# The last stage of a streaming block: two odd inner tiles moved from the first group to the end, and eight banks for the first up products

## The chip, the cores and the metric

The kernel runs on one core of a Trainium2 chip. The metric is device time in microseconds (us) of one execution. A core has a matrix engine (TensorE, "PE" in the profile, with its weight loads as "PEld"), three engines for elementwise work (VectorE "DVE", ScalarE "ACT", GpSimd "POOL"), and a sync engine (SP) that here issues the DMAs. PE writes only into PSUM, which has eight banks of 128 partitions by 512 float32. Data that the engines work on lies in SBUF.

## The reference

One block of a model with 1,024 tokens (plus 16 meta tokens, dropped at the end) and 1,024 channels: a mixer with two branches, and then a gated MLP with a causal depthwise convolution of width 3. The change touches the MLP only:

```python
def conv_ffn(hn, w_up, w_conv, w_down):
    u = hn @ w_up                                   # 1024 -> 2 * 2816
    u_pad = jnp.pad(u, ((0, 0), (CONV_W - 1, 0), (0, 0)))
    uc = sum(w_conv[j] * u_pad[:, j:j + length] for j in range(CONV_W))
    gate, val = jnp.split(uc, 2, axis=-1)
    return (jax.nn.silu(gate) * val) @ w_down       # 2816 -> 1024

h = h + conv_ffn(rms_norm(h, norm_ffn), ffn_up, ffn_conv, ffn_down)
return h[:, N_META:N_META + s]
```

## The kernel before

Every large product is done in float32 accuracy by three matmuls: both factors are split into a high part (rounded to the matrix engine's format) and a low part (the rest), and `mm3` (from L212) issues high x high (L218), high x low (L219) and low x high (L220) into one bank. A weight tile is split by `wload` (from L194): a DMA into `wf` (three buffers), a cast on ACT to `wh` (L205), a subtraction on POOL to `wl` (L206); `wh` and `wl` have four buffers each, and one such buffer holds four tiles of 128 by 128.

Stage 4 makes the mixer's output `h2` (eight tiles of 128 channels, held in SBUF to the end) and its normed and split form `x2`: 16 tiles, high and low for each of eight channel tiles. It does so in three windows of tokens; the last window is normed after the first two (L1038 on DVE, cast L1040 on ACT, subtraction L1041 on DVE or, for channel tiles 3 and 7, POOL).

Stage 5 is the MLP. The inner width of 2,816 is 22 tiles of 128. `up(kt)` makes one inner tile `gr`: for each of three windows of tokens a gate product and a value product (24 matmuls of 342 or 344 columns each, six products and 144 matmuls in all), each followed by the convolution (ACT L1137, DVE L1138 and L1139), Silu on ACT (L1149) and the product of both (DVE L1151). A product's bank comes free when L1139 has read it. The products use the tag `mm`, the down products the tag `dn`; `banks` says which PSUM banks a tag goes round.

Two inner tiles form a pair, and `seven_x` (ACT, DVE and POOL; L1102, L1103, L1106, L1109) makes from a pair seven left factors in the manner of Strassen: with inner tiles and output tiles taken two by two, and the tokens in two halves, seven products of 512 columns stand for eight. `seven_w` makes the weights that belong to them (adds on POOL L1076, casts on ACT L1083, subtractions on POOL L1084). `down(gi, gs, last)` adds a group's pairs into `h2`: for each of four pairs of output tiles seven products, each 3 matmuls per pair of inner tiles, and 12 additions of 128x512 on DVE (L1171). A group with one pair has 84 matmuls in its down products, a group with two pairs 168; both have 48 additions. `GS = [2, 4, 4, 4, 4, 4]` gives the inner tiles of each group: the first has one pair, the others two. A group's down products stand behind the first `up` of the next group; the last group's stand at the end, behind the last `up` and the last `seven_x`, and there each finished half of an output tile is sent out (L1176).

A scheduler fixes each engine's order when the program is built, from the written order and a modelled timeline. Each engine then works its own list strictly in order and waits on semaphores.

Of the kernel before, what the change touches and what calls it, by code (L numbers as in the profile page):

```python
# [8 lines left out]
F32R = mybir.dt.float32r  # L9
# [3 lines left out]
ALU = mybir.AluOpType  # L13
# [4 lines left out]
P = 128  # L18
D = 1024
KD = 8  # L20
SEQ = 1024
# [11 lines left out]
LT = L - T0  # L33
CW = [(14, 356), (356, 698), (698, 1040)]
CF = [(16, 356), (356, 698), (698, 1040)]
GS = [2, 4, 4, 4, 4, 4]
CHA = [(0, 348), (348, 696), (696, 1040)]
CV = [(0, 384), (384, 768), (768, 1040)]
G = [(0, 384), (384, 768), (768, 1040)]
# [154 lines left out]
def wload(S, src, kt, pool=None):  # L194

    nc = S.nc
    pool = pool or S.wp
    res = []
    for h in range(0, kt, 4):
        n = min(4, kt - h)  # L200
        wf = S.wp.tile([P, 4, P], F32, name="wf", tag="wf", bufs=3)
        nc.sync.dma_start(out=wf[:, :n], in_=src[:, h:h + n])
        wh = pool.tile([P, 4, P], F32R, name="wh", tag="wh", bufs=4)
        wl = pool.tile([P, 4, P], F32R, name="wl", tag="wl", bufs=4)
        nc.scalar.copy(out=wh[:, :n], in_=wf[:, :n])  # L205
        nc.gpsimd.tensor_tensor(out=wl[:, :n], in0=wf[:, :n], in1=wh[:, :n], op=ALU.subtract)  # L206
        for k in range(n):
            res.append((wh[:, k], wl[:, k]))
    return res


def mm3(S, ps, w, x, first=True, last=True):  # L212

    nc = S.nc
    n = len(w)
    for k in range(n):
        (wh, wl), (xh, xl) = w[k], x[k]
        nc.tensor.matmul(ps, lhsT=wh, rhs=xh, start=first and k == 0, stop=False)  # L218
        nc.tensor.matmul(ps, lhsT=wh, rhs=xl, start=False, stop=False)  # L219
        nc.tensor.matmul(ps, lhsT=wl, rhs=xh, start=False, stop=last and k == n - 1)  # L220
# [6 lines left out]
def banks(S, **use):  # L227

    S.psb.update({k: v.split() for k, v in use.items()})
    S.psn.update({k: 0 for k in use})  # L230


def slot(S, tag, name):
    w = 1024 if tag in "SM" else 512
    pool = S.pp if tag in "toAB" else S.pq
    return pool.tile([P, w], F32, name=name, tag=tag, bufs=1)


def psum(S, tag):

    slots = S.psb[tag]
    n = S.psn[tag] % len(slots)
    S.psn[tag] += 1
    t = slots[n]
    if n and slots[n - 1] == t:
        return S.half[tag][:, 512:1024]
    S.half[tag] = slot(S, t, tag)
    return S.half[tag][:, 0:512]
# [818 lines left out]
def seven_w(S, pool, w1, w2, n):  # L1067


    nc = S.nc  # L1070
    a11, a12 = w1[:, 0:2 * n:2], w1[:, 1:2 * n:2]
    a21, a22 = w2[:, 0:2 * n:2], w2[:, 1:2 * n:2]

    def add(x, y, op=ALU.add):
        t = pool.tile([P, 2, P], F32, name="ws", bufs=2)
        nc.gpsimd.tensor_tensor(out=t[:, :n], in0=x, in1=y, op=op)  # L1076
        return t[:, :n]

    def split(*src):
        wh, wl = [S.wp.tile([P, 4, P], F32R, name=nm, tag=nm, bufs=4) for nm in ("wh", "wl")]  # L1080
        for i, x in enumerate(src):
            o = slice(2 * i, 2 * i + n)
            nc.scalar.copy(out=wh[:, o], in_=x)  # L1083
            nc.gpsimd.tensor_tensor(out=wl[:, o], in0=x, in1=wh[:, o], op=ALU.subtract)  # L1084
        return [[(wh[:, 2 * i + k], wl[:, 2 * i + k]) for k in range(n)] for i in range(len(src))]

    yield from split(add(a11, a12), a22)
    yield from split(a11, add(a21, a22))
    yield from split(add(a11, a22), add(a12, a22, ALU.subtract))
    yield from split(add(a21, a11, ALU.subtract))  # L1090


def seven_x(S, g1, g2):


    nc = S.nc
    H = slice(0, 512), slice(512, 1024)
    T = lambda dt=F32R: S.xp.tile([P, SEQ], dt, name="gx", tag="x")

    def halves(g):  # L1100
        h, l = T(), T()
        nc.scalar.copy(out=h[:], in_=g[:])  # L1102
        nc.gpsimd.tensor_tensor(out=l[:], in0=g[:], in1=h[:], op=ALU.subtract)  # L1103
        return [(h[:, s], l[:, s]) for s in H]

    comb = lambda out, x, y, op=ALU.add: nc.vector.tensor_tensor(out=out, in0=x, in1=y, op=op)  # L1106
    (a, b), (c, d) = [[g[:, s] for s in H] for g in (g1, g2)]
    f = T()
    nc.scalar.copy(out=f[:, H[0]], in_=a)  # L1109
    comb(f[:, H[1]], a, f[:, H[0]], ALU.subtract)  # L1110
    u = T(F32)
    comb(u[:, H[0]], a, d)
    comb(u[:, H[1]], c, d)
    x1, x7 = halves(u)
    comb(c, c, a, ALU.subtract)
    x4, x5 = halves(g2)
    comb(a, a, b)
    comb(b, b, d, ALU.subtract)
    x6, x3 = halves(g1)
    return x5, x4, x3, (f[:, H[0]], f[:, H[1]]), x1, x7, x6  # L1120


def stage5(S):


    nc, tc = S.nc, S.tc
    banks(S, mm="0 1 2 3", dn="t o A B")
    with tc.tile_pool(name="p5", bufs=1) as p5:

        def conv(w, mt, a, z, name):  # L1130
            n = z - a
            c0 = a - 2 - T0
            ps = psum(S, "mm")
            mm3(S, ps[:, :n + 2], w, [(h[:, c0:c0 + n + 2], l[:, c0:c0 + n + 2]) for h, l in S.x2])
            cw = lambda j: S.par("conv", 44 * j + mt)
            t = p5.tile([P, 344], F32, name=name, bufs=2)
            nc.scalar.activation(out=t[:, :n], in_=ps[:, 0:n], func=AF.Identity, scale=cw(0))  # L1137
            nc.vector.scalar_tensor_tensor(out=t[:, :n], in0=ps[:, 1:1 + n], scalar=cw(1), in1=t[:, :n], op0=ALU.mult, op1=ALU.add)  # L1138
            nc.vector.scalar_tensor_tensor(out=t[:, :n], in0=ps[:, 2:2 + n], scalar=cw(2), in1=t[:, :n], op0=ALU.mult, op1=ALU.add)  # L1139
            return t  # L1140

        def up(kt):
            wg = wload(S, S.A["w_up"][kt], KD)
            wv = wload(S, S.A["w_up"][22 + kt], KD)
            gr = p5.tile([P, SEQ], F32, name="gr", bufs=2)
            for a, z in CF:
                n = z - a
                g = conv(wg, kt, a, z, "ug")
                nc.scalar.activation(out=g[:, :n], in_=g[:, :n], func=AF.Silu)  # L1149
                v = conv(wv, 22 + kt, a, z, "uv")  # L1150
                nc.vector.tensor_tensor(out=gr[:, a - N_META:z - N_META], in0=g[:, :n], in1=v[:, :n], op=ALU.mult)  # L1151
            return gr

        def down(gi, gs, last):
            k0 = sum(GS[:gi])
            n = len(gs)
            for m in range(0, KD, 2):
                wf = []
                for i in range(2):
                    w = S.wp.tile([P, 4, P], F32, name="wf", tag="wf", bufs=3)  # L1160
                    nc.sync.dma_start(out=w[:, :2 * n], in_=S.A["w_down"][m + i, :, k0:k0 + 2 * n])
                    wf.append(w)
                factors = seven_w(S, p5, wf[0], wf[1], n)
                half = lambda i, j: S.h2[m + i][:, 2 + 512 * j:514 + 512 * j]

                for j, to in enumerate((((0, 0, -1), (0, 1, 1)), ((0, 0, 1), (1, 0, 1)), ((0, 1, 1), (1, 1, 1)),
                                        ((1, 0, 1), (1, 1, -1)), ((0, 0, 1), (1, 1, 1)), ((0, 0, 1),), ((1, 1, 1),))):
                    ps = psum(S, "dn")
                    mm3(S, ps[:], next(factors), [g[j] for g in gs])
                    for r, c, sign in to:  # L1170
                        nc.vector.tensor_tensor(out=half(r, c), in0=half(r, c), in1=ps[:],  # L1171
                                                op=ALU.add if sign > 0 else ALU.subtract)
                if last:
                    for i in range(2):
                        for j in range(2):
                            nc.sync.dma_start(out=S.outT[m + i][:, 512 * j:512 * j + 512], in_=half(i, j))  # L1176

        pend = None
        kt = 0
        for gi, n in enumerate(GS):  # L1180
            gs = []
            for i in range(0, n, 2):
                g1 = up(kt)
                if i == 0 and pend is not None:
                    down(gi - 1, pend, False)
                g2 = up(kt + 1)
                kt += 2
                gs.append(seven_x(S, g1, g2))
            pend = gs
        down(len(GS) - 1, pend, True)  # L1190


def build(tc, A, outs):
# [114 lines left out]
```

## Time and profile before

| | |
|---|---|
| median of 3 runs | 1933.45 us (1931.68 to 1941.54) |
| the profiled execution | 1933.08 us, of which the span of the profile is 1930.9 us |
| PE busy | 1815.3 us, 94% of the span |
| DVE, ACT, POOL busy | 1114.6, 770.8, 766.7 us |
| mean granted TensorE clock | 0.969 |

The first up product of stage 5 starts at 1182.7 us of the span. PE is the busy engine there, so the profile is read by asking where PE, once stage 5 has begun, does not start its next matmul when it could. A matmul's own duration in the profile overlaps the next one's; what counts for throughput is the distance between starts.

### The profile page before, as it was taken

The page shows a single profiled execution, that of the slowest core. Times are in us where ns is not written, and L with a number is a line of the kernel's source. Part 1 is how long each engine was busy: PE and PEld are TensorE (multiplying, and loading weights), DVE is VectorE, ACT ScalarE, POOL GpSimd, SP SyncE. Part 2 cuts the span into 40 slices and gives each one's busy share as a digit, 9 for nine tenths or more (in the row PEclk, how much of TensorE's full clock was granted, in tenths as well). Part 3 has the DMA queues.
Part 4 walks back from the last instruction along what each step waited for, and adds up shares of the span by engine and source line. Part 5 has one row for each costly group of instructions (what it writes and reads, how often), then busy time and mean ns, then how long its engine had stood idle before and what let it go on. Part 6 is the DMA issues. An engine that isn't in the chain of part 4 may idle for free.

```text
span 1930.9 us, 33790 instructions
## 1 busy us (share of the span) xinstructions
PE 1815.3 (94%) x12744; PEld 1628.9 (84%) x12744; DVE 1114.6 (58%) x2062; ACT 770.8 (40%) x1706; POOL 766.7 (40%) x858
## 2 busy tenths in 40 slices
PE   6899999999998899999879998989999999999998
PEld 5588778788787688989769997979999899899996
DVE  6225635645727686442346447575756856757567
ACT  5345434444635432243365324333323333233232
POOL 4134224223324311232313334353744834636546
PEclk9899999899999899999989999999999999999998
DMA  5221331332413455565654332111121111211112
GB/s 183 95 71 44 83 77 55 79 88 57 112 47 90 95 138 154 156 188 160 188 147 137 111 123 84 36 53 44 44 67 44 44 46 43 66 44 44 61 39 104
DMA packets 197578, 170.84 MB, mean 88 GB/s; under 512 B 93768, under 2 KB 154744, under 8 KB 197416
## 3 DMA queue, kind: packets, MB, share of 16 engines
q1 hardware_dynamic: 197160, 168.62, 30.6%
q8 instruction: 101, 1.65, 0.4%
q14 instruction: 61, 0.50, 0.1%
q0 software_dynamic: 256, 0.07, 0.0%
HBM read 122.57 MB, written 46.06 MB: 87 GB/s over the span
## 4 chain that ended last, share of the span: by engine, by line
PE 54%; DVE 4%; DMA 2%; ACT 2%; issue 1%; POOL 1%; SPq 1%; DVEq 0%; ACTq 0%; POOLq 0%
PE mm L219 11%; PE mm L218 11%; PE mm L220 11%; PE dn L219 3%; PE dn L218 3%; PE dn L220 3%; PE gate L218 3%; PE gate L219 3%; PE gate L220 3%; DVE h L1171 1%; DMA y<-y_d 1%; DVE x L1041 1%; PE ch L541 1%; DVE x L1038 0%; PE ch L534 0%
## 5 line engine op out<-in xcount | busy, mean ns | idle before, releaser
L206 POOL TENSOR_TENSOR wl<-wf,wh 128x512 fp32r<-128x512 f32 x220 | 289.5, 1319 | 524.7 <-ACT wh L205 488.6
L218 PE MATMUL mm<-x,wh 128*128 128x344 f32 (+1 forms) x1056 | 338.3, 320 | 6.2 <-DVE ug L1139 6.2
L219 PE MATMUL mm<-x,wh 128*128 128x344 f32 (+1 forms) x1056 | 339.6, 322 | 0.0
L220 PE MATMUL mm<-x,wl 128*128 128x344 f32 (+1 forms) x1056 | 337.2, 320 | 1.0 <-POOL wl L206 1.0
L1171 DVE TENSOR_TENSOR h<-h,dn 128x512 f32<-128x512 f32 x288 | 183.3, 683 | 40.4 <-PE dn L220 32.8
L218 PEld LDWEIGHTS mm<-x,wh 128*128 128x128 f32 x1056 | 199.9, 189 | 7.1 <-ACT uv L1137 6.5
L205 ACT CAST wh<-wf 128x512 fp32r<-128x512 f32 x220 | 135.6, 617 | 164.8 <-PE mm L219 69.2
L220 PEld LDWEIGHTS mm<-x,wl 128*128 128x128 f32 x1056 | 199.4, 189 | 1.8 <-POOL wl L206 1.5
L219 PEld LDWEIGHTS mm<-x,wh 128*128 128x128 f32 x1056 | 200.0, 189 | 0.5
L218 PE MATMUL dn<-gx,wh 128*128 128x512 f32 x308 | 123.2, 401 | 11.1 <-ACT gx L1102 5.7
L218 PE MATMUL gate<-xh,wh 128*128 128x342 f32 x384 | 127.3, 332 | 4.1 <-ACT sg L856 2.1
L219 PE MATMUL gate<-xl,wh 128*128 128x342 f32 x384 | 127.3, 332 | 0.0
L220 PE MATMUL gate<-xh,wl 128*128 128x342 f32 x384 | 126.6, 330 | 0.0
L219 PE MATMUL dn<-gx,wh 128*128 128x512 f32 x308 | 122.6, 398 | 0.6 <-POOL gx L1103 0.6
L220 PE MATMUL dn<-gx,wl 128*128 128x512 f32 x308 | 122.1, 397 | 0.0
L218 PE MATMUL mm<-xh,wh 128*128 128x348 f32 (+5 forms) x336 | 116.9, 348 | 3.9 <-ACT xh L156 1.8
L219 PE MATMUL mm<-xl,wh 128*128 128x348 f32 (+5 forms) x336 | 114.4, 341 | 1.6 <-POOL xl L158 1.2
L220 PE MATMUL mm<-xh,wl 128*128 128x348 f32 (+5 forms) x336 | 112.6, 335 | 0.0
L1138 DVE SCALAR_TENSOR_TENSOR uv<-mm,par,uv 128x342 f32<-128x342 f32 (+1 forms) x66 | 37.7, 571 | 109.3 <-ACT uv L1137 109.3
L218 PE MATMUL pr<-xh,wh 128*128 128x386 f32 (+1 forms) x288 | 95.9, 333 | 1.4 <-ACT bt L469 1.4
L1084 POOL TENSOR_TENSOR wl<-ws,wh 128x256 fp32r<-128x256 f32 (+1 forms) x120 | 81.9, 694 | 33.5 <-ACT wh L1083 33.4
L219 PE MATMUL pr<-xl,wh 128*128 128x386 f32 (+1 forms) x288 | 94.8, 329 | 0.0
(317 smaller groups left out, 4333.1 us busy)
## 6 DMA issues: line engine op xcount, KB each, us to landing
wf<-in_w_up_dram SPq DMA_DIRECT2D x88, 256.0 KB, 2.7
wf<-in_w_down_dram SPq DMA_DIRECT2D x40, 256.0 KB, 2.8
sg_d<-sg SPq DMA_DIRECT2D x48, 171.0 KB, 3.4
sg<-sg_d SPq DMA_DIRECT2D x48, 171.0 KB, 2.4
wf<-in_w_gate_dram SPq DMA_DIRECT2D x32, 256.0 KB, 4.5
wf<-in_w_out_dram SPq DMA_DIRECT2D x32, 256.0 KB, 2.7
wf<-in_w_rw_dram SPq DMA_DIRECT2D x28, 256.0 KB, 2.8
wf<-in_w_qkv_dram SPq DMA_DIRECT2D x24, 256.0 KB, 2.8
```

The costliest lines, as they stand in the source:

```text
L205: nc.scalar.copy(out=wh[:, :n], in_=wf[:, :n])
L206: nc.gpsimd.tensor_tensor(out=wl[:, :n], in0=wf[:, :n], in1=wh[:, :n], op=ALU.subtract)
L218: nc.tensor.matmul(ps, lhsT=wh, rhs=xh, start=first and k == 0, stop=False)
L219: nc.tensor.matmul(ps, lhsT=wh, rhs=xl, start=False, stop=False)
L220: nc.tensor.matmul(ps, lhsT=wl, rhs=xh, start=False, stop=last and k == n - 1)
L541: nc.tensor.matmul(pz[r, q, :], lhsT=bkt[:, q, r], rhs=uv[e][:, q, :], start=True, stop=True)
L1041: (nc.gpsimd if m in (3, 7) else nc.vector).tensor_tensor(out=l[:, s], in0=x[:], in1=h[:, s], op=ALU.subtract)
L1084: nc.gpsimd.tensor_tensor(out=wl[:, o], in0=x, in1=wh[:, o], op=ALU.subtract)
L1138: nc.vector.scalar_tensor_tensor(out=t[:, :n], in0=ps[:, 1:1 + n], scalar=cw(1), in1=t[:, :n], op0=ALU.mult, op1=ALU.add)
L1171: nc.vector.tensor_tensor(out=half(r, c), in0=half(r, c), in1=ps[:], op=ALU.add if sign > 0 else ALU.subtract)
```

## The change

The group of one pair at the start goes. The first 20 inner tiles form five groups of two pairs. The last two inner tiles (20 and 21) are split into high and low as they are (`plain`) and multiplied by ordinary products (`down_last`), and their `up` calls stand ahead of the down products of the fifth group. The up products of the first two inner tiles may use all eight banks. The order in `up`, `seven_x` and `seven_w` is not touched.

```diff
-GS = [2, 4, 4, 4, 4, 4]
+GS = [4, 4, 4, 4, 4, 2]
...
-    banks(S, mm="0 1 2 3", dn="t o A B")
+    banks(S, mm="0 1 2 3 t o A B", dn="t o A B")
...
-        def down(gi, gs, last):
+        def down(gi, gs):
...
-                if last:
-                    for i in range(2):
-                        for j in range(2):
-                            nc.sync.dma_start(out=S.outT[m + i][:, 512 * j:512 * j + 512], in_=half(i, j))
+
+        def plain(g):
+
+            h, l = [S.mp.tile([P, SEQ], F32R, name="gp", tag="x2", bufs=16) for _ in range(2)]
+            nc.scalar.copy(out=h[:], in_=g[:])
+            nc.gpsimd.tensor_tensor(out=l[:], in0=g[:], in1=h[:], op=ALU.subtract)
+            return h, l
+
+        def down_last(gs):
+            for m in range(KD):
+                w = wload(S, S.A["w_down"][m, :, 20:22], 2)
+                for a in (0, 512):
+                    ps = psum(S, "dn")
+                    mm3(S, ps[:], w, [(h[:, a:a + 512], l[:, a:a + 512]) for h, l in gs])
+                    hs = S.h2[m][:, 2 + a:2 + a + 512]
+                    nc.vector.tensor_tensor(out=hs, in0=hs, in1=ps[:], op=ALU.add)
+                    nc.sync.dma_start(out=S.outT[m][:, a:a + 512], in_=hs)
...
-        for gi, n in enumerate(GS):
+        for gi in range(5):
             gs = []
-            for i in range(0, n, 2):
+            for i in range(2):
                 g1 = up(kt)
                 if i == 0 and pend is not None:
-                    down(gi - 1, pend, False)
+                    down(gi - 1, pend)
                 g2 = up(kt + 1)
                 kt += 2
                 gs.append(seven_x(S, g1, g2))
+                if kt == 2:
+                    banks(S, mm="0 1 2 3")
             pend = gs
-        down(len(GS) - 1, pend, True)
+        g1, g2 = up(20), up(21)
+        down(4, pend)
+        down_last([plain(g1), plain(g2)])
```

Three places show what the built order makes of it. First, PE at the third window of the first inner tile. `mm_13314` is its gate product, `mm_13344` its value product; x2_12045 and x2_12046 are the high and low part of channel tile 0, x2_12059 and x2_12060 of channel tile 7. Before, the end of the gate product and the start of the value product:

```order
L219 MATMUL mm_13314<-x2_12058,wh_13177 128x344
L220 MATMUL mm_13314<-x2_12057,wl_13178 128x344
L218 MATMUL mm_13314<-x2_12059,wh_13177 128x344
L219 MATMUL mm_13314<-x2_12060,wh_13177 128x344
L220 MATMUL mm_13314<-x2_12059,wl_13178 128x344
L218 MATMUL mm_13344<-x2_12045,wh_13183 128x344
L219 MATMUL mm_13344<-x2_12046,wh_13183 128x344
L220 MATMUL mm_13344<-x2_12045,wl_13184 128x344
```

And now, at the start of the gate product:

```order
L219 MATMUL mm_13284<-x2_12060,wh_13189 128x344
L220 MATMUL mm_13284<-x2_12059,wl_13190 128x344
L218 MATMUL mm_13314<-x2_12045,wh_13171 128x344
L218 MATMUL mm_13344<-x2_12045,wh_13183 128x344
L219 MATMUL mm_13314<-x2_12046,wh_13171 128x344
L220 MATMUL mm_13314<-x2_12045,wl_13172 128x344
L218 MATMUL mm_13314<-x2_12047,wh_13171 128x344
L219 MATMUL mm_13344<-x2_12046,wh_13183 128x344
L220 MATMUL mm_13344<-x2_12045,wl_13184 128x344
L218 MATMUL mm_13344<-x2_12047,wh_13183 128x344
```

The two products have moved into one another: they go through the channel tiles together, in two banks.

Second, ACT at the same place. `ug_13219` and the three below it are the first four products, read from their banks; `wh_13376` and `wh_13382` are the gate weights of the second inner tile, `wh_13388` and `wh_13394` its value weights. Before:

```order
L1040 CAST x2_12059<-x_13161 128x342
L1137 ACTIVATE ug_13219<-mm_13194,par_136 128x340
L1137 ACTIVATE uv_13249<-mm_13224,par_136 128x340
L1137 ACTIVATE ug_13279<-mm_13254,par_136 128x342
L1137 ACTIVATE uv_13309<-mm_13284,par_136 128x342
L1149 ACT_TABLE_LOAD
L1149 ACTIVATE ug_13219<-ug_13219 128x340
L1149 ACTIVATE ug_13279<-ug_13279 128x342
L1109 CAST gx_13579<-gr_13193 128x512
L205 CAST wh_13376<-wf_13374 128x512
L205 CAST wh_13382<-wf_13380 128x512
```

And now:

```order
L1040 CAST x2_12059<-x_13161 128x342
L205 CAST wh_13376<-wf_13374 128x512
L205 CAST wh_13382<-wf_13380 128x512
L1137 ACTIVATE ug_13219<-mm_13194,par_136 128x340
L1137 ACTIVATE uv_13249<-mm_13224,par_136 128x340
L1137 ACTIVATE ug_13279<-mm_13254,par_136 128x342
L1137 ACTIVATE uv_13309<-mm_13284,par_136 128x342
L1149 ACT_TABLE_LOAD
L1149 ACTIVATE ug_13219<-ug_13219 128x340
L205 CAST wh_13388<-wf_13386 128x512
L205 CAST wh_13394<-wf_13392 128x512
```

The casts of the second inner tile's gate weights have moved ahead of the first four reads of a bank.

Third, POOL around the last `up`. `wf_...` with 128x256 operands are the down weights of the first pair of output tiles. Before, with the three subtractions of `seven_x` (L1103) of the last pair:

```order
L1076 TENSOR_TENSOR ws_19872<-wf_19867 128x256
L1076 TENSOR_TENSOR ws_19898<-wf_19869 128x256
L1103 TENSOR_TENSOR gx_19752<-gx_19748,gx_19751 128x1024
L1103 TENSOR_TENSOR gx_19757<-gr_19564,gx_19756 128x1024
L1103 TENSOR_TENSOR gx_19763<-gr_19359,gx_19762 128x1024
L1084 TENSOR_TENSOR wl_19875<-ws_19872,wh_19874 128x256
L1084 TENSOR_TENSOR wl_19875<-wf_19869,wh_19874 128x256
```

And now, where those three stand an `up` pair earlier and the two subtractions of `plain` (L1178) have come in:

```order
L1084 TENSOR_TENSOR wl_19475<-wf_19441,wh_19474 128x256
L1084 TENSOR_TENSOR wl_19475<-ws_19472,wh_19474 128x256
L1178 TENSOR_TENSOR gp_19830<-gr_19055,gp_19829 128x1024
L1076 TENSOR_TENSOR ws_19500<-wf_19441,wf_19443 128x256
L1084 TENSOR_TENSOR wl_19503<-ws_19498,wh_19502 128x256
L1084 TENSOR_TENSOR wl_19503<-ws_19500,wh_19502 128x256
L1076 TENSOR_TENSOR ws_19525<-wf_19443,wf_19441 128x256
L1076 TENSOR_TENSOR ws_19543<-wf_19538 128x256
L1178 TENSOR_TENSOR gp_19834<-gr_19260,gp_19833 128x1024
L1084 TENSOR_TENSOR wl_19528<-ws_19525,wh_19527 128x256
L1084 TENSOR_TENSOR wl_19546<-ws_19543,wh_19545 128x256
```

The weights of products 0 to 3 of the first pair of output tiles stand ahead of the first L1178, those of products 4 and 5 (`wl_19503`) between the two, those of product 6 (`wl_19528`) behind the second.

## Rows read from the trace of the kernel before

**Rows 1.** PE's waits by what released them, 1175 to 1310 us: total, times, longest.
```profile
PE mm L218 <- DVE ug L1139: 6.2, 1, 6.2
PE dn L218 <- ACT wh L1083: 2.7, 4, 1.3
PE dn L218 <- DVE h L1171: 2.5, 5, 0.9
```
**Rows 2.** The same view, 1310 us to the end: its larger row of two.
```profile
PE dn L218 <- ACT gx L1102: 5.7, 2, 3.6
```
**Rows 3.** Down matmuls, 1896 to 1927 us, undisturbed: count, ns min/median/max, first and last start.
```profile
L218 PE MATMUL dn<-gx,wh x44: 388/392/399, 1895.8 to 1925.7; 128*128 128x512 f32 x44
```
**Rows 4.** Up matmuls in the same view, 1296.5 to 1380 us, undisturbed.
```profile
L218 PE MATMUL mm<-x,wh x177: 313/319/328, 1296.6 to 1379.9; 128*128 128x344 f32 x121, 128*128 128x342 f32 x56
```
**Rows 5.** PE in order of time, 1200 to 1212 us: start, duration; in brackets, idle before.
```profile
1200.62 0.32 PE L220 MATMUL mm<-x,wl 128*128 128x344 f32 x1
1207.19 0.63 PE L218 MATMUL mm<-x,wh 128*128 128x344 f32 x1 [6.25 <-DVE ug L1139]
...
1211.01 0.32 PE L219 MATMUL mm<-x,wh 128*128 128x344 f32 x1
```
**Rows 6.** All engines by stretch; the column behind POOL's is the granted clock.
```profile
1205.00:1210.00 5.00, 2.81 (x10) 2.84 (x11) 4.38 (x10) 4.05 (x7) 0.00 (x0) 0.50 0.00 0
1885.00:1890.00 5.00, 2.60 (x5) 1.27 (x5) 1.83 (x1) 1.04 (x1) 5.00 (x3) 0.50 0.00 0
```
**Rows 7.** POOL, ACT and DVE in order of time, 1203 to 1207 us.
```profile
1203.99 0.91 POOL L1041 TENSOR_TENSOR x<-x,x 128x342 fp32r<-128x342 f32 x1 [2.44 <-ACT x L1040]
...
1204.93 0.54 ACT L1137 ACTIVATE ug<-mm,par 128x340 f32<-128x340 f32 x1 [1.02 <-POOL x L1041]
...
1206.48 0.56 DVE L1139 SCALAR_TENSOR_TENSOR ug<-mm,par,ug 128x340 f32<-128x340 f32 x1
...
1206.81 1.28 ACT L1149 ACT_TABLE_LOAD   x1
```
**Rows 8.** Matmuls of the first group's down products, 1255 to 1300 us, as in rows 3.
```profile
L218 PE MATMUL dn<-gx,wh x28: 388/401/496, 1262.0 to 1293.5; 128*128 128x512 f32 x28
```
**Rows 9.** DVE's groups, 1255 to 1295 us: count, busy us, mean ns, idle before.
```profile
L1171 DVE TENSOR_TENSOR h<-h,dn 128x512 f32<-128x512 f32 x48 | 29.5, 680 | 3.1 <-PE dn L220 2.9
```
**Rows 10.** PE in order of time, 1877 us to the end.
```profile
1877.40 0.39 PE L218 MATMUL dn<-gx,wh 128*128 128x512 f32 x1
...
1926.14 0.40 PE L220 MATMUL dn<-gx,wl 128*128 128x512 f32 x1
```
**Rows 11.** DVE and POOL in order of time, 1879 to 1891 us.
```profile
1879.40 0.93 DVE L1151 TENSOR_TENSOR gr<-ug,uv 128x342 f32<-128x342 f32 x1
...
1883.76 2.52 POOL L1103 TENSOR_TENSOR gx<-gx 128x1024 fp32r<-128x1024 f32 x1 [1.70 <-ACT gx L1102]
1886.24 5.15 POOL L1103 TENSOR_TENSOR gx<-gr,gx 128x1024 fp32r<-128x1024 f32 x2
```
**Rows 12.** Groups of DVE, POOL and ACT, 1896 to 1926 us, as in rows 9.
```profile
L1171 DVE TENSOR_TENSOR h<-h,dn 128x512 f32<-128x512 f32 x38 | 24.7, 685 | 5.4 <-PE dn L220 3.8
...
L1084 POOL TENSOR_TENSOR wl<-ws,wh 128x256 fp32r<-128x256 f32 x13 | 9.5, 739 | 2.4 <-ACT wh L1083 2.4
...
L1083 ACT CAST wh<-ws 128x256 fp32r<-128x256 f32 x13 | 5.2, 406 | 14.8 <-PE dn L219 9.2 <-POOL ws L1076 5.4
```
**Rows 13.** DMA issues, 1880 us to the end: count, KB each, median us to landing.
```profile
out_dram<-h SPq DMA_DIRECT2D x16, 256.0 KB, 2.0
wf<-in_w_down_dram SPq DMA_DIRECT2D x3, 256.0 KB, 3.1
```
**Rows 14.** DVE at 1218 us, then POOL and DVE at 1252 us, in order of time.
```profile
1218.95 0.52 DVE L1151 TENSOR_TENSOR gr<-ug,uv 128x342 f32<-128x342 f32 x1
...
1251.88 2.38 POOL L1103 TENSOR_TENSOR gx<-gr,gx 128x1024 fp32r<-128x1024 f32 x1 [1.71 <-ACT gx L1102]
1251.91 2.72 DVE L1151 TENSOR_TENSOR gr<-ug,uv 128x340 f32<-128x340 f32 x1
```

## The prediction

> **What bounds the kernel now.** I read the page's busy lines first: PE is the busy engine, and in stage 5 it has hardly a pause. Then PE's waits, in two stretches of stage 5. Up to 1310 us there is one long wait of an up product for DVE, which must give a bank back, and there are nine short waits of down products, for weights from ACT and for DVE's additions [rows 1]. From there to the end only the last `seven_x` makes PE wait, 5.7 us on ACT and 0.6 us on POOL [rows 2]. So stage 5 loses time in three places, all of which the change touches.
>
> A wait row counts neither the slow clock after a pause nor small delays between matmuls, so I size the losses by starts. Undisturbed, 43 steps of three down matmuls take 29.9 us, 0.232 us each [rows 3]; 176 steps of three up matmuls take 83.3 us, 0.158 us each [rows 4]. What a stretch takes beyond its matmuls at these distances is lost.
>
> - *Start.* Four products are done by 1200.78 us (the last start plus 0.158); the fifth starts at 1207.19, so 6.4 us pass. The 13 matmuls up to 1211.01 take 3.8 us instead of 2.1 [rows 5], since the granted clock there is 0.50, the lower level of 1.2 GHz [rows 6]. Lost: 6.4 + 1.7 = 8.1 us.
> - *First down products.* They run from 1262.0 to about 1294.2 us (the last L218 at 1293.5 plus three steps) [rows 8], 32.2 us. In there stand 84 of them and, by the order of before, 27 up matmuls: 84 x 0.232 + 27 x 0.158 = 23.8 us. Lost: 8.4 us. The cause is on DVE: 48 additions at 0.68 us [rows 9] are 8.2 us per pair of output tiles, and PE needs for its 21 matmuls only 4.9 us. With two pairs of inner tiles PE needs 42 x 0.232 = 9.7 us for the same 8.2 us of DVE.
> - *Last `seven_x`.* 168 down matmuls start from 1877.40 to 1926.14 us [rows 10]: 49.0 us with the last, against 168 x 0.232 = 39.0. Lost: 10.0 us, part of it again at a clock of 0.50 [rows 6].
>
> **The change part by part.**
>
> *The first group of one pair goes.* All five remaining Strassen groups have two pairs, and for such groups rows 2 show no wait on DVE or on down weights anywhere after 1310 us. I take the whole 8.4 us. The bounds: 8.2 us of additions per 9.7 us leave DVE 1.5 us per pair of output tiles for the up work that falls in, as it does in before's later groups; at worst half is lost again, 4 us.
>
> *The last two tiles move behind the fifth group.* `seven_x` of tiles 18 and 19 then has two `up` calls, 288 matmuls or 45 us of PE, beside it; in before its POOL part took 7.7 us [rows 11]. Ahead of the fifth group's down products no `seven_x` is late, so the 10.0 us go. What is late next is the weights. POOL has two new subtractions of 128x1024, for which the nearest rows give 2.5 us each [rows 11]. By the new order the first stands behind the weights of products 0 to 3 and the second ahead of those of product 6. From the last up matmul (call it 0) PE reaches product 6 after 6 x 6 x 0.232 = 8.4 us. On POOL the first subtraction can run before 0, since `gr` of tile 20 is long ready and the storage it takes is read for the last time in the first matmuls of the last product, 3.8 us before 0. The second needs the last piece of `gr`; from the same moment in before that is about 3 us (L1151 ends at 1880.3 [rows 11], PE's first down matmul starts at 1877.4 [rows 10]), with the two additions now ahead of it on DVE 3.4, the cast of 128x1024 1.0, the subtraction 2.5, one weight subtraction 0.74 [rows 12]: 7.7 us. It fits with 0.7 us to spare. After that POOL needs 12 x 0.74 = 8.9 us per pair of output tiles against PE's 9.7 and recovers. I take 0.5 us; the bounds are 0 and the two subtractions in full, 5.
>
> *Twelve more matmuls.* The last two tiles took 7 x 4 x 3 = 84 down matmuls as a Strassen group and take 8 x 2 x 2 x 3 = 96 now: 12 x 0.232 = 2.8 us, on the path. DVE has 16 additions instead of 48 there, 1.4 us per output tile beside 2.8 us on PE. The eight weight tiles go the known way (DMA, cast, subtraction) with three buffers ahead, so they hide behind 2.8 us per tile; and the output leaves as 16 transfers of 256 KB, 2.0 us to landing each [rows 13], two per 2.8 us. The last one leaves after the last addition as before, so the end behind the last matmul stays.
>
> *Eight banks at the start.* The gate and value product of the third window no longer wait for a bank. They are fed as the window's normed tiles come; the last is ready at 1204.9 us (POOL's end) [rows 7], and PE, in step through both products, asks for it at 1200.78 + 42 x 0.158 = 1207.4. So PE runs through and is done at 1208.4. New waits: ACT now casts the second tile's gate weights ahead of its first four reads of a bank, and the second cast needs weights that the gate product reads to about 1208.1. The first read so moves from 1204.93 to about 1208.7, and the first bank comes free, as in rows 7 some 2.1 us later, at 1210.8. PE asks for it (the ninth product, in the first bank again) at about 1208.4 + 12 x 0.158 = 1210.3: 0.5 us. The value weights are cast behind the table load of 1.28 us [rows 7], another 0.5 us. So 1.0 us of the 8.1 comes back; bounds 0 and all 8.1, if the wait is long enough for the clock to fall again.
>
> *Sum.* -8.1 + 1.0 - 8.4 - 10.0 + 0.5 + 2.8 = -22.2 us. The profiled execution took 1933.08 us, 2.2 more than its span, and lies 0.4 below the median of the runs: 1933.1 - 22.2 = 1910.9; I say 1911.
>
> A rule that speaks against the new POOL work: DVE's product L1151, 0.52 us by itself, took 2.72 us where POOL ran a subtraction of 2.38 us [rows 14], while DVE's additions out of a bank kept to 0.685 us beside a POOL at work [rows 12]. The Trainium skill, SBUF — State Buffer, section "SBUF: two separate sides", says that a VectorE instruction with two SBUF inputs and a GpSimd instruction that reads SBUF take a shared pair of ports as an exclusive lock, and the loser waits for the whole instruction; by that the trace agrees for L1151, and the additions, one of whose inputs is a bank, are spared. If the last L1151 met the first new subtraction, it would be late by up to 2.2 us (2.72 - 0.52), and product 6 by 1.5 us. That is inside the bounds above and belongs to the first rival.
>
> **The rivals.**
>
> - *POOL is late in the fifth group.* For it: 8.9 of 9.7 us leave little room, and the two subtractions and a blocked L1151 come to 7.2 us at the moment when four weight buffers are all the lead there is. Against it: in rows 12 POOL still waits for ACT, and ACT for PE to release a buffer, so POOL runs ahead there. It costs 3 to 7 us more: 1914 to 1918.
> - *The start gives nothing.* The bank wait turns into waits for weights and reads behind ACT's early casts, the clock falls again, and the 7.1 us stay lost: 1918. For it: the order on ACT; against: the sums above leave waits of half a microsecond.
> - *The waits come back elsewhere* in the four more ups before the first down products or between the groups, by 13 us or more: 1924 to 1938, no change. Nothing after 1310 us speaks for it [rows 2].
> - *The last eight weight tiles are not loaded ahead: slower.* If only one is in flight at a time, each output tile waits 3.1 us for its DMA [rows 13], 0.41 for the cast and 0.74 for the subtraction [rows 12]: 8 x 4.2 = 34 us on top, 1945. It decides as soon as load, cast and subtraction of one tile cannot overlap the matmuls of the one before; with two in flight 4.2 us stand against 5.6 and are hidden. Three `wf` buffers speak against it.
>
> **How the numbers follow.** The forecast 0.62, POOL late 0.16, the start without gain 0.14, no change 0.04, slower 0.04. The forecast's own range is the sum with small errors of each term, 1907 to 1914; the two milder rivals end at 1918. The range 1906 to 1918 leaves out the last two cases and a little on either side. A difference under 0.5% (9.7 us) can hardly be told from no change: faster 0.92, same 0.04, slower 0.04.
>
> **What would show it.** At the third window PE has no idle of more than 1 us and the granted clock stays at 1.00; the first down products follow one another at 0.232 us with two pairs; behind the last up matmul 264 down matmuls take 61.2 to 62 us, with the small wait, if any, at product 6 and for POOL's weights. It is wrong if PE waits for `wh` or `wl` for more than 3 us there, if additions pace a down group, if the eight tiles at the end start further apart than 2.8 us, or if the end behind the last matmul grows beyond 4.5 us.

## The result and the profile after

| | before | after |
|---|---|---|
| median of 6 runs | 1936.8 us (1931.68 to 1943.78) | 1914.55 us (1908.85 to 1922.32) |
| profiled execution, its span | 1933.08, 1930.9 us | 1909.92, 1908.1 us |
| first up product of stage 5 to the span's end | 748.2 us | 724.7 us |
| PE busy, share of the span | 1815.3 us, 94% | 1809.4 us, 95% |

The ratio of the times is 0.989, with a 95% interval of 0.9866 to 0.9914: faster by 1.1%. The prediction was 1911 us, in a range of 1906 to 1918. Against the profiled execution of before its sum was -22.2 us; the profiled executions lie 23.2 apart, 23.5 of it in stage 5 (the stages ahead took 0.7 longer, and what lies around the span 0.4 less). The medians lie 22.3 apart; that the median after is 3.6 above 1911 comes from the other side, since before's median over six runs is 1936.8 and not the 1933.45 of the first three. Where runs differ by a few us I compare the third line of the table, since the stages ahead vary by more than that (last section).

PE's waits in the kernel after, from 1175 us to the end of the span (total, times, longest), are these two rows and no more:

```profile
PE mm L220 <- POOL wl L206: 1.8, 3, 0.9
PE mm L218 <- ACT wh L205: 0.6, 1, 0.6
```

Every row of [rows 1, 2] is gone. The waits that are left lie within 6 us of the stage's start, two of the four ahead of it, and were there before.

**Start.** First the stretches of 5 us at the third window and in the first down products (PE's busy time and count first, the granted clock behind POOL's column), then ACT and DVE in order of time:

```profile
1205.00:1210.00 5.00, 5.00 (x34) 5.00 (x33) 3.33 (x7) 4.92 (x9) 3.19 (x3) 1.00 0.25 78
1300.00:1340.00 40.00, 40.00 (x177) 32.57 (x176) 32.48 (x51) 11.70 (x28) 32.73 (x45) 1.00 0.21 66
```
```profile
1205.05 1.14 ACT L205 CAST wh<-wf 128x512 fp32r<-128x512 f32 x2 [0.40 <-PE mm L219]
...
1206.10 0.54 ACT L1137 ACTIVATE ug<-mm,par 128x340 f32<-128x340 f32 x1
...
1207.63 0.56 DVE L1139 SCALAR_TENSOR_TENSOR ug<-mm,par,ug 128x340 f32<-128x340 f32 x1
```

Where PE stood for 6 us and then ran at half the clock [rows 5, 6], it is busy for all 5 us at a granted clock of 1.00. ACT reads the first bank at 1206.10 and DVE gives it back at 1208.19 (1207.63 + 0.56).

**Down products.** The matmuls of the fifth group and of the last two inner tiles (count, ns min/median/max, first and last start):

```profile
L218 PE MATMUL dn<-gx,wh x56: 387/394/399, 1842.2 to 1880.5; 128*128 128x512 f32 x56
...
L218 PE MATMUL dn<-gp,wh x32: 389/394/396, 1881.2 to 1902.9; 128*128 128x512 f32 x32
```

And the last matmul and the last addition in order of time:

```profile
1903.36 0.39 PE L220 MATMUL dn<-gp,wl 128*128 128x512 f32 x1
1903.79 0.69 DVE L1188 TENSOR_TENSOR h<-h,dn 128x512 f32<-128x512 f32 x1 [0.71 <-PE dn L220]
```

From 1842.2 us, 264 matmuls take 1903.36 + 0.23 - 1842.2 = 61.4 us; at 0.232 each that is 61.2. Nothing is lost where [rows 8] lost 8.4 us and [rows 10] 10.0. From the last matmul's slot to the span's end it is 4.5 us, as before. The first group's down products, now with two pairs, fill the stretch of 1300 to 1340 us above: 177 matmuls, a few up matmuls among them, and no pause.

### The profile page after: what moved, and what is told of

Its sections match the earlier page's. It is cut to its first block, busy times and chain, and to the rows that moved or that the text cites. A ratio compares the mean times of both kernels' runs of the same rounds, so it can differ in the third digit from the quotient of the medians.

```text
span 1908.1 us, 33665 instructions
## 1 busy us (share of the span) xinstructions
PE 1809.4 (95%) x12756; PEld 1629.3 (85%) x12756; DVE 1086.0 (57%) x2024; ACT 764.4 (40%) x1684; POOL 748.4 (39%) x817
## 4 chain that ended last, share of the span: by engine, by line
PE 57%; DVE 2%; DMA 2%; ACT 1%; POOL 1%; issue 1%; SPq 1%; ACTq 0%; DVEq 0%; POOLq 0%
PE mm L218 11%; PE mm L219 11%; PE mm L220 11%; PE dn L220 4%; PE dn L218 4%; PE dn L219 4%; PE gate L218 3%; PE gate L219 3%; PE gate L220 3%; DMA y<-y_d 1%; PE ch L541 1%; PE ch L534 0%; PE ch L523 0%; PE ch L551 0%; PE ch L549 0%
## 5 line engine op out<-in xcount | busy, mean ns | idle before, releaser
L206 POOL TENSOR_TENSOR wl<-wf,wh 128x512 fp32r<-128x512 f32 (+1 forms) x228 | 295.9, 1301 | 532.7 <-ACT wh L205 520.1
L219 PE MATMUL mm<-x,wh 128*128 128x344 f32 (+1 forms) x1056 | 338.5, 321 | 0.0
L220 PE MATMUL mm<-x,wl 128*128 128x344 f32 (+1 forms) x1056 | 336.9, 320 | 0.9 <-POOL wl L206 0.9
L218 PE MATMUL mm<-x,wh 128*128 128x344 f32 (+1 forms) x1056 | 336.6, 320 | 0.0
L205 ACT CAST wh<-wf 128x512 fp32r<-128x512 f32 (+1 forms) x228 | 138.7, 610 | 175.7 <-PE mm L219 70.4
L220 PEld LDWEIGHTS mm<-x,wl 128*128 128x128 f32 x1056 | 198.9, 189 | 1.7 <-POOL wl L206 1.5
L219 PEld LDWEIGHTS mm<-x,wh 128*128 128x128 f32 x1056 | 199.2, 189 | 0.4
L218 PEld LDWEIGHTS mm<-x,wh 128*128 128x128 f32 x1056 | 199.0, 189 | 0.5
L1171 DVE TENSOR_TENSOR h<-h,dn 128x512 f32<-128x512 f32 x240 | 153.1, 683 | 34.9 <-PE dn L220 28.6
L218 PE MATMUL gate<-xh,wh 128*128 128x342 f32 x384 | 127.4, 332 | 4.6 <-ACT sg L856 2.3
L219 PE MATMUL gate<-xl,wh 128*128 128x342 f32 x384 | 127.2, 331 | 0.0
L220 PE MATMUL gate<-xh,wl 128*128 128x342 f32 x384 | 126.6, 330 | 0.0
L218 PE MATMUL mm<-xh,wh 128*128 128x348 f32 (+5 forms) x336 | 116.9, 348 | 4.1 <-DVE sg L269 1.9
L219 PE MATMUL mm<-xl,wh 128*128 128x348 f32 (+5 forms) x336 | 113.9, 339 | 1.8 <-POOL xl L158 1.2
L220 PE MATMUL mm<-xh,wl 128*128 128x348 f32 (+5 forms) x336 | 112.5, 335 | 0.0
L218 PE MATMUL dn<-gx,wh 128*128 128x512 f32 x280 | 110.3, 394 | 0.0
L219 PE MATMUL dn<-gx,wh 128*128 128x512 f32 x280 | 110.2, 393 | 0.0
L220 PE MATMUL dn<-gx,wl 128*128 128x512 f32 x280 | 109.8, 394 | 0.0
L218 PE MATMUL pr<-xh,wh 128*128 128x386 f32 (+1 forms) x288 | 95.9, 333 | 1.4 <-ACT bt L469 1.4
L220 PE MATMUL pr<-xh,wl 128*128 128x386 f32 (+1 forms) x288 | 94.8, 329 | 0.0
L219 PE MATMUL pr<-xl,wh 128*128 128x386 f32 (+1 forms) x288 | 94.8, 329 | 0.0
```

## The experiments

"Length" is the time from the first up product of stage 5 to the end of the span, in the profiled execution; every ratio is to runs of the kernel before that were timed beside it (their medians: 1936.96 us for e1 to e4, 1935.92 for e5 to e7).

| | length, us | median, us | ratio, 95% interval |
|---|---|---|---|
| before | 748.2 | 1936.8 | |
| after | 724.7 | 1914.55 | 0.989 (0.9866 to 0.9914) |
| e1_four_banks | 733.1 | 1918.93 | 0.992 (0.9895 to 0.9945) |
| e2_banks_only | 740.7 | 1927.67 | 0.9957 (0.9934 to 0.9979) |
| e3_last_pair_seven | 734.1 | 1917.63 | 0.9914 (0.9888 to 0.9939) |
| e4_down_first | 727.4 | 1917.61 | 0.9917 (0.9892 to 0.9941) |
| e5_pair_at_end | 751.1 | 1937.18 | 1.0018 (0.9987 to 1.0049) |
| e6_one_buffer | 724.8 | 1910.98 | 0.9866 (0.98 to 0.9932) |
| e7_pool_twice | 727.4 | 1916.65 | 0.9895 (0.9829 to 0.9962) |

The intervals reach some 5 us to either side (6 for e5; 13 for e6 and e7, which were timed twice each), too far for terms of 3 us. By the ratios e1, e3 and e4 are 4.6 to 5.8 us longer than the kernel after, uncertain by some 7 us. The lengths and the waits tell them apart. Each length is that of one execution; where no edit reaches, they repeat closely: a group of 168 down matmuls between undisturbed `up` calls takes 40.1 to 40.3 us in all nine.

### The eight banks, taken away and by themselves

e1_four_banks, the kernel after without them:

```diff
-    banks(S, mm="0 1 2 3 t o A B", dn="t o A B")
+    banks(S, mm="0 1 2 3", dn="t o A B")
```

> The changed kernel with four banks for the first up products, as before. If the start's loss was the wait for a bank and the slow clock behind it, it all comes back: one wait of about 6.2 us on DVE L1139 before the fifth product, a granted clock of 0.50 around it, and a span 8.1 us longer, 1916.2 instead of 1908.1 us. Rival: the third window's normed tiles come too late for the banks to matter (the wait would then show the normed tiles as what released it); span within 1.5 us of 1908.1.

Measured: the length grows by 8.4 us. PE's waits for DVE, and a stretch behind that wait:

```profile
PE mm L218 <- DVE ug L1139: 6.3, 1, 6.3
```
```profile
1220.00:1225.00 5.00, 2.00 (x7) 2.03 (x8) 3.67 (x8) 3.81 (x7) 0.72 (x1) 0.54 0.00 0
```

It is the wait of [rows 1] again, with the granted clock down after it as in [rows 6]; this start lies some 15 us later in its span. What released PE was DVE and not the normed tiles, so the rival is out.

e2_banks_only, the kernel before with them (and back to four banks behind the second inner tile):

```diff
-    banks(S, mm="0 1 2 3", dn="t o A B")
+    banks(S, mm="0 1 2 3 t o A B", dn="t o A B")
...
+                if kt == 2:
+                    banks(S, mm="0 1 2 3")
```

> The kernel before with the eight banks for its first two up products and nothing else. If the three losses are independent, only the first goes: span 1930.9 - 8.1 = 1922.8 us, the waits of the first down products (some 5 us) and of the last seven_x (6.3 us) as before. Rival: the gain at the start is given back at the first down products, where DVE is the slow engine and now gets its work earlier; span 1928 to 1931.

Measured: 7.5 us shorter than before. PE's waits from 1175 us to the end, the three largest, all in down products:

```profile
PE dn L218 <- ACT gx L1102: 6.2, 2, 3.6
PE dn L218 <- DVE h L1171: 3.0, 5, 0.9
PE dn L218 <- ACT wh L1083: 1.9, 4, 1.3
```

The bank wait has gone and the others stand. From the first up product to the first down product the kernel is 8.1 us faster; 0.6 of that is lost again in the down products (the first group's take 31.8 us in place of 32.2, the last group's 50.0 in place of 49.0). So the start by itself is worth 8.1 to 8.4 us, from either side.

### The last pair: its place, its form, its order

e5_pair_at_end, the kernel before with only the order of groups changed:

```diff
-GS = [2, 4, 4, 4, 4, 4]
+GS = [4, 4, 4, 4, 4, 2]
```

> The kernel before with nothing changed but the place of the group of one pair: at the end, as a Strassen pair behind the last seven_x, four banks. The stages ahead of the MLP vary by some us from run to run, so this and the next runs are judged by the time from the first up product to the end: 748.2 us before, 724.7 changed. If each loss has its own cause, the first group's 8.4 us go, but at the end the late seven_x (10.0 us) leaves PE without the 15 matmuls of another pair (3.5 us) and the additions then pace the 84 matmuls (32.9 us instead of 19.5): 748.2 - 8.4 + 3.5 + 13.4 = 756.7, slower than before. Rival: the place of the small group was all; 739.8.

Measured: 2.9 us longer than before, and by the times no change. PE's larger waits from 1310 us on, and a stretch at the last `seven_x`:

```profile
PE dn L218 <- ACT gx L1102: 7.3, 2, 5.3
PE dn L218 <- DVE h L1171: 2.4, 5, 0.9
```
```profile
1890.00:1895.00 5.00, 1.22 (x2) 0.50 (x2) 3.90 (x3) 2.77 (x3) 4.09 (x2) 0.64 0.00 0
```

The first group, with two pairs, waits for nothing. The additions pace the last group instead, and the last `seven_x` makes PE wait longer, up to 5.3 us at once against 3.6 [rows 2]. The last 84 matmuls take 38.0 us, 18.5 more than 84 x 0.232 = 19.5: just the 8.4 and the 10.0 us of before, now in one place, and the end behind the last matmul grows by 2.0 us. I had expected 8.5 us more than before: right in kind, too large in size, since I let both losses grow where they meet. The move alone gives nothing; it takes the loss along.

e3_last_pair_seven, the kernel after with the last pair as a Strassen group behind the fifth group's down products:

```diff
...
-        down_last([plain(g1), plain(g2)])
+        gs = [seven_x(S, g1, g2, lambda dt=F32R: S.mp.tile([P, SEQ], dt, name="gx", tag="x2", bufs=16))]
+        down(5, gs)
+        for m in range(KD):
+            for j in range(2):
+                nc.sync.dma_start(out=S.outT[m][:, 512 * j:512 * j + 512], in_=S.h2[m][:, 2 + 512 * j:514 + 512 * j])
```

> The changed kernel with its last two inner tiles as a Strassen pair (84 matmuls, 48 additions) in place of ordinary products (96 matmuls, 16 additions); their seven_x runs beside the fifth group's down products, its tiles in the storage that the normed tiles leave. If additions pace a group of one pair, it takes 48 x 0.685 = 32.9 us instead of 96 x 0.232 = 22.3: span about 1908.1 + 10.6 = 1918.7, up to 1924 if seven_x also delays the fifth group (DVE has 1.5 us to spare per pair of output tiles there). Rival: the number of matmuls decides: 12 x 0.232 = 2.8 us shorter, 1905.3.

Measured: 9.4 us longer than after, though PE has 12 matmuls fewer. PE's waits from 1310 us on, the first matmul of the last pair and the last of all, and DVE's additions from 1880 to 1918 us (count, busy us, mean ns):

```profile
PE dn L218 <- DVE h L1171: 4.6, 7, 0.9
PE dn L218 <- ACT wh L1083: 1.3, 4, 0.6
```
```profile
1885.07 0.39 PE L218 MATMUL dn<-gx,wh 128*128 128x512 f32 x1
...
1911.87 0.40 PE L220 MATMUL dn<-gx,wl 128*128 128x512 f32 x1
```
```profile
L1171 DVE TENSOR_TENSOR h<-h,dn 128x512 f32<-128x512 f32 x57 | 34.6, 680 | 0.9 <-PE dn L220 0.7
```

Here is the first group's disease at the end: the additions keep DVE busy for 34.6 of these 38 us, the 84 matmuls of the last pair take 27.0 us (1911.87 + 0.23 - 1885.07) where 19.5 would do, and the end behind the last matmul grows from 4.5 to 6.5 us (1918.6 - 1911.87 - 0.23). Against the 96 ordinary matmuls and their 22.4 us in the kernel after that is 4.6 + 2.0 us. The other 2.9 us are not the additions of this pair: the fifth group's down products, with the extra `seven_x` beside them, take 41.9 us in place of 39.0 (two of the seven waits for DVE and one of 0.6 us for ACT lie there). So the ordinary form of the last two tiles, with 2.8 us more on PE, is worth 9.4 us: some 6.6 by its 16 additions in place of 48, and 2.9 in the fifth group, beside which no other `seven_x` then runs.

e4_down_first, the kernel after with the last `up` behind the fifth group's down products:

```diff
-        g1, g2 = up(20), up(21)
+        g1 = up(20)
         down(4, pend)
+        g2 = up(21)
```

> The changed kernel with the fifth group's down products between the up products of tiles 20 and 21, where a group's down products stand elsewhere; the ordinary products follow the last up directly. If the order was worth the cover it gives, PE now waits for the end of the last gr (2.9 us), the cast (1.0) and the subtraction (2.5), about 6.4 us behind the last up matmul, less some 12 matmuls that need only tile 20 (2.8 us): 3.6 us and 1 to 2 us of slow clock, span 1912 to 1914. Rival: after ordinary products little is late, and the order is worth nothing: within 1 us of 1908.1.

Measured: 2.7 us longer, less than expected. PE, ACT and POOL behind the last up product, in order of time:

```profile
1894.95 0.40 PE L220 MATMUL dn<-gp,wl 128*128 128x512 f32 x1
1895.14 1.04 ACT L1177 CAST gp<-gr 128x1024 fp32r<-128x1024 f32 x1 [1.80 <-DVE gr L1151]
1896.24 1.19 PE L218 MATMUL dn<-gp,wh 128*128 128x512 f32 x4 [0.89 <-ACT gp L1177]
1896.26 2.42 POOL L1178 TENSOR_TENSOR gp<-gr,gp 128x1024 fp32r<-128x1024 f32 x1 [1.94 <-ACT gp L1177]
1898.73 0.50 PE L219 MATMUL dn<-gp,wh 128*128 128x512 f32 x1 [1.30 <-POOL gp L1178]
```

The last tile's split is late, cast and subtraction one behind the other: PE idles for 0.89 and 1.30 us. I had counted the 12 matmuls of tile 20 that PE runs first, but not tile 21's four high x high matmuls during the subtraction (0.9 us of the 3.6), and 1 to 2 us of slow clock did not come: the granted clock is 1.00 in 1890 to 1900 us.

### The cover for the new work: POOL, and the last weights

e7_pool_twice, the kernel after with each of the two subtractions of `plain` done twice:

```diff
-            nc.gpsimd.tensor_tensor(out=l[:], in0=g[:], in1=h[:], op=ALU.subtract)
+            for _ in range(2):
+                nc.gpsimd.tensor_tensor(out=l[:], in0=g[:], in1=h[:], op=ALU.subtract)
```

> The changed kernel with each of the two new POOL subtractions done twice (the second time to the same place): 2 x 2.4 us more for POOL ahead of the fifth group's weights. In the changed kernel the weights of product 6 are ready at 1850.4 us and PE's product 6 is due at 1850.5, so if the step fits as narrowly as that, all of it comes to PE: 4.7 us, 729.4 us from the first up product to the end, with waits of PE on POOL wl L1084. Rival: the buffered weights hide it; within 1 us of 724.7.

Measured: 2.7 us longer for 4.9 us more of POOL. The place in order of time (SP's row is a DMA issue):

```profile
1849.15 0.74 POOL L1076 TENSOR_TENSOR ws<-wf 128x256 f32<-128x256 f32 x1
...
1849.92 0.80 SPq L1161 DMA_DIRECT2D wf<-in_w_down_dram  x2
...
1853.80 0.40 ACT L1083 CAST wh<-wf 128x256 fp32r<-128x256 f32 x1 [3.46 <-DMA wf<-in_w_down_dram]
...
1854.25 0.50 PE L218 MATMUL dn<-gx,wh 128*128 128x512 f32 x1 [1.61 <-ACT wh L1083]
```

The wait is not the one I named. PE waits for a cast, the cast for a DMA, and the DMA starts 0.03 us after POOL has read its buffer for the last time (1849.15 + 0.74). So a late POOL reaches PE through the next weights' load. In the kernel after that DMA starts at 1845.80 us; with the start of stage 5 1.5 us later here, it is 2.6 us late, about the first repeat (2.4 us); no wait of PE shows the second.

PE loses about as much, but the two are not one number. The cast behind the DMA ends at 1854.20 us, 3.8 us late (in the kernel after at 1848.94), since the load, too, took longer: 3.9 us from its issue to the cast, against 2.7. In the kernel after this cast is 3.5 us ahead of the matmul that reads it (1852.40), so 0.3 us would have been left. But the built order of e7 has also changed: PE reads these weights six matmuls, or 1.4 us, sooner. Together that is 1.7 us, the wait of 1.61. The late buffer is shown, its price for an unchanged order is not; and where PE loses the rest of the 2.7 us I have not followed up.

e6_one_buffer, the kernel after with a single buffer for the last eight weight tiles' DMAs:

```diff
-                w = wload(S, S.A["w_down"][m, :, 20:22], 2)
+                wf = p5.tile([P, 2, P], F32, name="wf1", bufs=1)
+                nc.sync.dma_start(out=wf[:], in_=S.A["w_down"][m, :, 20:22])
...
```

> The changed kernel with one buffer in place of three for the last eight weight tiles. As the prediction's slower case has it, each of them would wait for its own load, cast and subtraction: 8 x 4.2 = 34 us more, 759 from the first up product to the end. Against that: with one buffer the next load still begins once the subtraction has read the last one, so that it runs beside 2.8 us of matmuls, and only what the chain of about 3.6 us takes beyond 2.8 us accumulates, less the 4 to 5 us by which the first tile is early: 1.5 to 5 us more, 726 to 730.

Measured: 0.1 us. ACT's casts of these weights, the first and the last of eight, and then PE's products with the last tile, in order of time:

```profile
1873.91 0.41 ACT L1186 CAST wh<-wf 128x256 fp32r<-128x256 f32 x1 [0.84 <-PE dn L219]
...
1898.36 0.41 ACT L1186 CAST wh<-wf 128x256 fp32r<-128x256 f32 x1 [3.06 <-DMA wf<-in_w_down_dram]
```
```profile
1899.32 0.40 PE L219 MATMUL dn<-gp,wh 128*128 128x512 f32 x1
1899.64 0.50 PE L220 MATMUL dn<-gp,wl 128*128 128x512 f32 x1
```

One tile at a time takes 24.45 / 7 = 3.5 us (the casts lie 24.45 us apart), more than PE's 2.8. But the first tile's low part is ready at 1875.1 us (the cast's start plus 0.41 and a subtraction of 0.74), and PE reads it first at 1879.95: a lead of 4.9 us. Seven tiles at 0.7 us use up 4.9. The lead lasts just to the last tile, where PE is 0.1 us late (0.32 between the two starts in place of 0.23). I had expected 1.5 to 5 us: the chain of 3.5 us and the lead of 4.9 were each a little better than I had put them.

## Why the prediction was right, point by point

| term | predicted, us | measured, us |
|---|---|---|
| start, lost before | -8.1 | -8.4 (e1), -8.1 (e2, up to the first down product) |
| start, given back | +1.0 | 0 |
| first group's additions | -8.4 | all of it: no wait left |
| last `seven_x` | -10.0 | all of it: no wait left |
| POOL at product 6 | +0.5 | 0 |
| twelve more matmuls | +2.8 | +2.8, by the count and the distance |
| end behind the last matmul | 0 | 0 (4.5 and 4.5) |

Without the two gains given back the sum is -8.1 - 8.4 - 10.0 + 2.8 = -23.7 us; the length of stage 5 fell by 23.5.

- *The three losses and what each was made of* were right, and each comes back when its cause is put back: e1 for the banks, e3 for the 48 additions per single pair, e5 for the `seven_x` with nothing beside it. That the two losses of down products do not go by moving the pair (e5) shows that the place alone does not do the work. What does is the ordinary form and the order of the `up` calls, but not as two terms that add up: e5 and e1 both have four banks, and e5 is 18.0 us longer; the form by itself is worth 9.4 us of that (e3), the order by itself 2.7 (e4). The rest shows only where both are undone and PE waits for `gx`. Whether ordinary products at the start, in place of the end, would do as well was not run.
- *The +1.0 at the start was mis-sized.* The step was that the second cast of the next weights needs weights that the gate product reads to 1208.1, and so ACT's first read of a bank comes at 1208.7. It came at 1206.10, and both casts were through by 1206.2. The step had the wrong storage: in the built program `wh_13382` lies where `wh_13183` lay, the value product's first weights, and not where `wh_13177` lay, the gate product's second. In the interwoven order `wh_13183` is read for the last time by the 24th of the window's 48 matmuls, while the gate's second weights are read to about 1208.8. PE's 24th, and its first matmul into the first bank again:

```profile
1205.17 0.32 PE L219 MATMUL mm<-x,wh 128*128 128x344 f32 x1
...
1211.34 0.32 PE L218 MATMUL mm<-x,wh 128*128 128x344 f32 x1
```

  The bank was so free at 1208.19 in place of 1210.8, 3.2 us before PE came to it at 1211.34. The other half, 0.5 us for the value weights cast behind the table load, did not come either: no wait of PE for `wh` lies in stage 5. So nothing came back at the start, for a reason that the prediction did not have and the built program could have told.
- *The +0.5 for POOL was in place, and nothing of it was paid.* In order of time, from the last product of tile 21 on DVE to PE's first matmul with the low weights of product 6:

```profile
1845.03 1.72 POOL L1076 TENSOR_TENSOR ws<-wf 128x256 f32<-128x256 f32 x2
1845.28 0.87 DVE L1151 TENSOR_TENSOR gr<-ug,uv 128x342 f32<-128x342 f32 x1
...
1847.31 2.44 POOL L1178 TENSOR_TENSOR gp<-gr,gp 128x1024 fp32r<-128x1024 f32 x1 [0.56 <-ACT gp L1177]
...
1849.71 1.43 POOL L1084 TENSOR_TENSOR wl<-ws,wh 128x256 fp32r<-128x256 f32 x2
...
1851.47 0.40 PE L220 MATMUL dn<-gx,wl 128*128 128x512 f32 x1
```

  Counted from PE's first down matmul at 1842.20, POOL's first weight subtraction for product 6 ends at about 8.2 us (half of the row's 1.43 behind 1849.71) where I had 7.7. PE starts product 6 at 8.3, where I had 8.4. But its L218 and L219 read only the high weights; the low ones are first read by its L220, in the built order the fifth matmul from there, at 9.3 us. I had compared with the start of the product (and did so again for e7). So 1.0 us was to spare, not 0.7: POOL ended 0.5 later than I had it, and the need came 0.9 later.
- *The rule on the shared ports.* L1151 took 0.87 us beside POOL's additions (L1076), against 0.52 by itself [rows 14]. In e7 it met the repeat of the first new subtraction:

```profile
1845.80 2.42 POOL L1179 TENSOR_TENSOR gp<-gr,gp 128x1024 fp32r<-128x1024 f32 x1
1846.75 1.84 DVE L1151 TENSOR_TENSOR gr<-ug,uv 128x342 f32<-128x342 f32 x1
```

  By the Trainium skill, SBUF — State Buffer, section "SBUF: two separate sides", the loser waits for the other's whole instruction. The traces agree in all three meetings: L1151 lasts as long as what was left of POOL's instruction plus 0.37 or 0.38 us. Of the 2.38 us in [rows 14] 2.35 were left, and it took 2.72; in e7 1.47 were left, and it took 1.84; here 0.49 of an L1076 of 0.74 us, and it took 0.87. That it met a short one, and not the 2.4 us of L1178, is why the 2.2 us of the first rival did not come; e7 shows 1.3 of them.
- *The slower rival's mechanism is possible, its price was wrong.* It charged eight whole load chains, 34 us. e6 makes the loads wait for one another, and the time does not change. A chain that is slower than PE costs only what it takes beyond PE per tile, less its lead: 7 x 0.7 - 4.9, which is nothing.
- *The two other rivals did not come.* The start gave its 8.1 us (e1, e2), and no wait came back elsewhere: the two wait rows of the kernel after are all there is.

## What to carry to other kernels

Before you price a write that must wait for a reader, look up in the built program whose storage it takes, and which matmul reads it last or first. An elementwise pass whose size does not shrink with the group (here 48 additions, 33 us, whether PE has 84 matmuls or 168) sets how small a group may be; for the odd rest a plainer form with more matmuls can be the faster one, and putting the rest elsewhere only moves the wait. Put the up products of the last tiles ahead of down products that are ready, so that the last tiles are prepared beside matmuls and not with PE empty (2.7 us here, e4). Price a load chain that is too slow by its excess per step less its lead, and look for a late engine's effect where it gives a buffer back, not only where it delivers.

## What the runs showed of the hardware that was not expected

The stages ahead of stage 5 are the same in the kernels compared, and yet stage 5 began between 1179.1 (e5) and 1198.5 us (e1). The granted clock goes with it. In the stretch of 200 to 300 us it is 0.86 in the two executions that reached stage 5 last (e4 at 1194.6, e1 at 1198.5) and 0.96 to 0.98 in the seven others (1179.1 to 1185.5). This stretch in the kernel after and in e1_four_banks (PE's count, and the clock behind POOL's column):

```profile
200.00:300.00 100.00, 94.23 (x772) 79.11 (x772) 47.57 (x119) 40.48 (x109) 23.07 (x33) 0.96 0.34 86
```
```profile
200.00:300.00 100.00, 94.73 (x719) 76.94 (x719) 46.44 (x115) 38.54 (x104) 20.89 (x31) 0.86 0.31 76
```

PE is as busy, but at a mean clock of 0.86 it starts 719 matmuls in place of 772. Why the clock was lower in those two these runs do not tell. Thirteen executions of the kernel before, timed beside e5 to e7, had spans from 1928.5 us at a mean clock of 0.97 to 1944.7 us at 0.959. A spread of 16 us is more than any of the three gains here, which is why lengths within the stage were compared and not times alone.
